# Three more 4 KB tiles from a smaller descriptor memory, and new tables for the first 224 steps of a diffusion-transformer kernel

## The chip, the cores and the metric

The kernel runs on one core of a Trainium2 chip. TensorE (PE) multiplies, VectorE (DVE) and ScalarE (ACT) work on tiles, GpSimd (POOL) and SyncE (SP) start transfers. The metric is the device time of one execution in microseconds (us), given as the median of three runs. A profile of one execution comes with it.

## The reference

One layer of a hybrid diffusion transformer is computed in fp32 for two groups of 128 tokens (a prompt and a sample), with D = 2048 and D_FF = 8192:

- adaLN: (shift1, scale1, gate1, shift2, scale2, gate2) = SiLU(c) @ w_ada + b_ada, one vector per group
- h = RMSNorm(x) * (1 + scale1) + shift1; one projection p = h @ w_in gives q, k, v of two attention mixers and two gates
- mixer A (windowed, grouped heads) and mixer B (neighbourhood attention with a position bias), both also over cached keys
- merged = sigmoid(gate_A) * (o_A @ w_br_a) + sigmoid(gate_B) * (o_B @ w_br_b); x = x + gate1 * (merged @ w_out)
- x = x + gate2 * (relu(h2 @ w_up)^2 @ w_down), with h2 from RMSNorm, shift2 and scale2

## The kernel before

**Steps.** All large products are cut into some 450 steps. A step has one weight tile of 128x1024 fp32 (512 KB). SP loads it (`raw`, L255), ACT copies it into a rounded high part `wH` (`copy`, L103, called from `prep`), DVE subtracts to get the low part `wL` (L281), and PE runs 12 matmuls of 128x512: high x high, low weight x high, and high x low of the activations, for two token groups and two slices of the contraction. The matmul lines differ by stage: L599 to L601 in the first three steps, L463 to L465 in `start_steps`, L498 to L500 in `products`, L332 to L334 later. Steps are counted from 0 here.

**Order.** Nothing is scheduled at run time. `run` (L305) writes the program out step by step: before step i it issues the loads of the steps up to i + RUN[i], prepares (`prep_to`) the tiles up to step i + LOOK[i], writes the 12 matmuls, and then the functions that `at` has hung on step i. Each engine runs its own instructions in the order in which they were written, so a digit of LOOK decides how many subtractions DVE has ahead of what step i hangs on it. LO_DMA lists steps whose `wL` comes another way: ACT copies `wH` with a factor of -1 and POOL starts a transfer that adds the weights to it (L287, L288).

**What is hung on the steps.** `mod_pair` (five groups of adaLN columns; the first, in `begin`, is narrower) loads eight tiles `araw` of 512 KB, multiplies them with the conditioning vector on PE (`wide_mm`, L366) into one PSUM bank, has ACT copy the sum to `S` (`ada_evac`), and PE transposes `S` four times (`ada_cols`, L380, `ps_sel`). One step later `make_h` and one more later `split_h` make the activations of the next slice. DOTS and its kin place dot products on DVE (L1499, two of them to a tile `aT`) for the other adaLN columns. POST, JOBS and SS_AT place the work of the attention.

**Chunks.** The input projection begins while only some slices of h are known: `start_steps` runs each unit of 512 columns over a chunk of h and puts the partial sum away. SEED1 says for each unit and chunk how the parts are joined: "1" lets ACT copy the earlier part into the PSUM banks beforehand (a seed), "0" lets DVE add it afterwards (L476). The sums live in pairs of banks from a pool of four (`pacc`, L87), so a step that opens a new sum takes a pair that one of the last two sums held, and waits until that has been copied or added away.

**Tiles.** Weights, their two parts, `araw`, `aT` and most activations are tiles of 4 KB per partition. They come from one pool with GEN = 50 rotating buffers under one tag.

Of the kernel before, what the change touches and what calls it, by code (L numbers as in the profile page):

```python
# [10 lines left out]
F32 = mybir.dt.float32  # L11
F32R = mybir.dt.float32r
# [18 lines left out]
GEN = 50  # L31
# [4 lines left out]
FILL = {1: [("gB", 2), ("gB", 3)], 3: [("gB", 0), ("gB", 1)]}  # L36
DOTS1 = [9, 11, 14, 19, 22, 24, 25, 27, 28, 30, 32, 33, 34, 35, 37, 40, 41, 42, 44, 46, 48, 49, 51, 53]
# [9 lines left out]
SEED1 = "111110100100111111011111111001011111"  # L47
# [4 lines left out]
LO_DMA = [50, 54, 56, 63, 77, 107, 129, 144, 145, 176, 184, 188, 189, 203, 228, 233, 250, 286, 297, 360, 388, 392, 403, 447]  # L52
LO_AHEAD = 2

LOOK = "610013015100121312024402233324102425654224523344556654121016645565652437574377445343425661516353205100022636320000411134203644154134500458230315565645456443574337324421522555644666784051000205311111322534111433455554321045445111013410444324654734331001335565775443654453304436533423355423455542233213213545587654334232213213202440122544412433432313432443523324313211333435533333213331314344422557756822145342656433332302254541454475574464555546763333345544"
RUN = "345110004667224234111350007998421004464200022565595544243214333434399864346555377654224635443144230021224242114401324515201346530331035587986564665545676867644543555342013141147676676965699967265287998988511453877787785653022200123446553345324545104653232464345673321110102122521121211202355533232133432223443232410110000000011234344212022112531112752123301000112323643331133410100122454235566436675432012021222210010001154457832224556577677636445664422134"
CONST_AT = [83, 79]
XL_DMA = [8]
HI_DMA = []
ADA_AT = [None, 4, 13, 22, 25]  # L60
XS_AT = {1: 3, 2: 24, 3: 34}
POST = {('kvA', 0): [81, 83, 89], ('qA', 0): [84, 86, 92], ('qA', 1): [84, 86, 90], ('kB', 0): [88, 92, 98], ('qB', 0): [94, 100, 104], ('kB', 1): [98, 101, 103], ('qB', 1): [102, 106, 107]}
JOBS = [[93, 94, 95, 100, 106], [93, 94, 99, 104, 106], [98, 98, 100, 105, 114], [101, 104, 107, 110, 111], [107, 107, 110, 115, 118], [109, 109, 111, 118, 121], [113, 114, 115, 126, 128], [116, 116, 119, 122, 124]]
# [9 lines left out]
M_AT = [4, 6, 9]  # L73
# [7 lines left out]
def tile_hybrid_step(ctx: ExitStack, tc: tile.TileContext, a):  # L81
# [20 lines left out]
    def copy(out, in_):  # L102
        act.activation(out, in_, AF.Copy)  # L103
# [6 lines left out]
    cols = cp.tile([P, 172], F32, name="cols")[:, 0:164]  # L110
# [20 lines left out]
    wr = G("wr", F32R)  # L131

    def warm_r(*forms):

        for m, v in forms:
            pe.matmul(ps_warm[0:m, 0:v.shape[-1]], wr[:, 0:m], v, start=True, stop=True)

# [11 lines left out]
    for h in range(2):  # L149
        copy(wr[:, 512 * h:512 * h + 512], wm)  # L150
# [154 lines left out]
    def run():  # L305
        loads.sort(key=lambda x: x[:2])
        for st in wsteps:
            while loads and loads[0][0] <= st["i"] + int(RUN[st["i"]]):
                loads.pop(0)[2]()
# [3 lines left out]
            to = st["i"] + int(LOOK[st["i"]]) + 1  # L313
# [255 lines left out]
    def begin():  # L569
# [49 lines left out]
        warm_r(*[(P, wr[:, 0:512])] * 3, *[(P, wr[:, 8:520])] * 3)  # L619
# [1060 lines left out]
```

## Time and profile before

| | |
|---|---|
| runs | 1313.8, 1313.86, 1314.27 us, median 1313.86 us |
| profiled execution | 1313.68 us, of which the span is 1311.8 us |
| PE busy | 1298.4 us (99%) |
| DVE busy | 1146.1 us (87%) |
| ACT busy | 917.5 us (70%) |
| POOL busy | 58.5 us (4%) |
| mean read and write rate | 300 GB/s |

Times in the profile count from the start of the span. The 1.9 us between the span and the execution lie outside it. A row of the view over time gives start, duration, engine, line, operation, output <- inputs, shape and count, and in brackets how long the engine had been idle and which instruction ended that. Rows of the view of waits give an instruction, what it waited for, the sum in us, how often, and the longest. A window row gives the window, its length, and for each engine the busy time and the number of instructions, then the granted clock of PE, the busy share of the DMA engines and the rate. The 128x512 matmuls are pipelined: a row shows 0.39 us for one, but the next starts 0.227 us later, so a step of 12 takes 2.72 us.

### The profile page before, as it was taken

How to read it: one execution, taken by the hardware profiler on the slowest of the kernel's cores; microseconds unless marked ns; L12 is line 12 of the kernel's file. 1: busy time of each engine (PE TensorE's matmuls, PEld its weight loads, DVE VectorE, ACT ScalarE, POOL GpSimd, SP SyncE). 2: the span in 40 equal slices, each digit the busy share in tenths (PEclk: the TensorE clock that was granted, in tenths of full speed). 3: DMA queues.
4: the chain of work that ended last, by engine and by line, in shares of the span. 5: the costliest groups of instructions: out<-in, count | busy, mean ns of one | idle time of the engine just before them, and what ended most of it. 6: DMA issues, size and time to landing. Idle time of an engine off the chain costs nothing.

```text
span 1311.8 us, 17435 instructions
## 1 busy us (share of the span) xinstructions
PE 1298.4 (99%) x5978; PEld 1052.2 (80%) x5978; DVE 1146.1 (87%) x1532; ACT 917.5 (70%) x1289; POOL 58.5 (4%) x67
## 2 busy tenths in 40 slices
PE   8999999999999999999999999999999999999998
PEld 4767888888777778888888888888888888888886
DVE  4578999999899999999879998897989999979653
ACT  5657766689765657645687857869678787796881
POOL 0000000341100000000000000000000000000000
PEclk9999999999999999999999999999999999999999
DMA  9999998897889999999399775788586696968692
GB/s 379 418 411 420 361 365 320 306 364 278 290 347 365 419 384 330 369 344 372 113 321 317 244 256 179 273 293 282 201 297 224 212 317 248 297 161 304 204 345 78
DMA packets 148313, 393.80 MB, mean 300 GB/s; under 512 B 51680, under 2 KB 52672, under 8 KB 148224
## 3 DMA queue, kind: packets, MB, share of 16 engines
q1 hardware_dynamic: 144064, 378.18, 77.7%
q0 software_dynamic: 4016, 14.42, 5.7%
q8 instruction: 47, 0.77, 0.2%
q14 instruction: 42, 0.34, 0.1%
q10 hardware_dynamic: 144, 0.08, 0.0%
HBM read 373.97 MB, written 8.70 MB: 292 GB/s over the span
## 4 chain that ended last, share of the span: by engine, by line
PE 70%; DVE 3%; ACT 0%; issue 0%; DVEq 0%; ACTq 0%
PE acc L332 14%; PE acc L333 14%; PE acc L334 14%; PE Q L1281 6%; PE Q L1283 6%; PE Q L1282 6%; PE Z L1281 1%; PE Z L1283 1%; PE Z L1282 1%; DVE aT L1499 1%; DVE junk L1499 1%; PE acc L1119 1%; PE acc L1120 1%; PE acc L1102 1%; PE acc L1101 1%; PE acc L1103 1%
## 5 line engine op out<-in xcount | busy, mean ns | idle before, releaser
L281 DVE TENSOR_TENSOR wL<-raw,wH 128x1024 fp32r<-128x1024 f32 x361 | 425.7, 1224 | 62.4 <-ACT wH L103 61.8
L103 ACT ACTIVATE wH<-raw 128x1024 fp32r<-128x1024 f32 (+1 forms) x391 | 387.4, 1043 | 49.7 <-PE acc L334 10.2
L1499 DVE SCALAR_TENSOR_TENSOR aT<-aT,cB 128x1024 f32<-128x1024 f32 x144 | 173.9, 1224 | 1.1
L1499 DVE SCALAR_TENSOR_TENSOR junk<-aT,cB 128x1024 bf16<-128x1024 f32 x144 | 173.9, 1224 | 0.0
L463 PE MATMUL acc<-wH,hH 128*128 128x512 f32 x276 | 108.2, 392 | 0.0
L465 PE MATMUL acc<-wH,hL 128*128 128x512 f32 x276 | 107.5, 389 | 0.0
L464 PE MATMUL acc<-wL,hH 128*128 128x512 f32 x276 | 107.5, 389 | 0.0
L103 ACT ACTIVATE uH<-raw 128x1024 fp32r<-128x1024 f32 x34 | 36.1, 1063 | 65.7 <-DVE raw L1345 57.9
L463 PEld LDWEIGHTS acc<-wH,hH 128*128 128x128 f32 x276 | 51.8, 188 | 13.8 <-issue 2.5
L465 PEld LDWEIGHTS acc<-wH,hL 128*128 128x128 f32 x276 | 51.8, 188 | 10.9
L464 PEld LDWEIGHTS acc<-wL,hH 128*128 128x128 f32 x276 | 51.8, 188 | 10.6
L103 ACT ACTIVATE tH<-t 128x1024 fp32r<-128x1024 f32 x34 | 36.0, 1058 | 28.7 <-DVE t L1338 26.5
L332 PE MATMUL acc<-wH,hH 128*128 128x512 f32 x128 | 52.6, 411 | 0.0
L333 PE MATMUL acc<-wL,hH 128*128 128x512 f32 x128 | 50.1, 392 | 1.3 <-DVE wL L281 1.3
L498 PE MATMUL acc<-wH,hH 128*128 128x512 f32 x128 | 50.5, 394 | 0.0
L499 PE MATMUL acc<-wL,hH 128*128 128x512 f32 x128 | 49.9, 390 | 0.1
L334 PE MATMUL acc<-wH,hL 128*128 128x512 f32 x128 | 50.1, 391 | 0.0
L500 PE MATMUL acc<-wH,hL 128*128 128x512 f32 x128 | 50.0, 390 | 0.0
L1348 DVE TENSOR_TENSOR uL<-raw,uH 128x1024 fp32r<-128x1024 f32 x34 | 41.7, 1226 | 1.4 <-ACT uH L103 0.3
L103 ACT ACTIVATE acc<-dsum 128x512 f32<-128x512 f32 x56 | 31.7, 590 | 15.7 <-DVE t L1067 8.3
L1338 DVE TENSOR_TENSOR t<-raw 128x1024 f32<-128x1024 f32 x34 | 41.4, 1219 | 1.3 <-PE Q L1282 1.3
L1347 DVE TENSOR_TENSOR tL<-t,tH 128x1024 fp32r<-128x1024 f32 x34 | 41.4, 1219 | 0.0
(652 smaller groups left out, 3331.9 us busy)
## 6 DMA issues: line engine op xcount, KB each, us to landing
raw<-in_w_in SPq DMA_DIRECT2D x133, 512.0 KB, 7.6
raw<-in_w_down SPq DMA_DIRECT2D x128, 512.0 KB, 6.3
aT<-in_w_adaT SPq DMA_DIRECT2D x80, 512.0 KB, 8.0
raw<-in_w_upF SPq DMA_DIRECT2D x68, 512.0 KB, 5.4
aT<-in_w_gT SPq DMA_DIRECT2D x64, 512.0 KB, 7.7
raw<-in_w_up SPq DMA_DIRECT2D x60, 512.0 KB, 6.2
araw<-in_w_pair SPq DMA_DIRECT2D x48, 512.0 KB, 8.9
raw<-in_w_out SPq DMA_DIRECT2D x32, 512.0 KB, 9.2
```

Of the source, the lines that this page charges most:

```text
L103: act.activation(out, in_, AF.Copy)
L281: dve.tensor_tensor(st["lo"], st["raw"], st["hi"].bitcast(F32), op=OP.subtract)
L332: pe.matmul(acc[tb], sh, wh[:, k, :], start=f, stop=False, skip_group_check=seeded)
L333: pe.matmul(acc[tb], sh, wl[:, k, :], start=False, stop=False, skip_group_check=seeded)
L334: pe.matmul(acc[tb], sl, wh[:, k, :], start=False, stop=l, skip_group_check=seeded)
L463: pe.matmul(acc[tb], sh, wh[:, k, :], start=opened[u] and k == 0, stop=False, skip_group_check=skip)
L464: pe.matmul(acc[tb], sh, wl[:, k, :], start=False, stop=False, skip_group_check=skip)
L465: pe.matmul(acc[tb], sl, wh[:, k, :], start=False, stop=last and k == 1, skip_group_check=skip)
L1281: pe.matmul(acc, stat[0], hi, start=f, stop=False)
L1282: pe.matmul(acc, stat[0], lo, start=False, stop=False)
L1283: pe.matmul(acc, stat[1], hi, start=False, stop=l)
L1499: dve.scalar_tensor_tensor(out, box["raw"], 1.0, cB[s, tag], op0=OP.mult, op1=OP.mult, accum_out=dst[:, s, fb:fb + 1])
```

## The change

- The memory that POOL uses for the descriptors of its transfers is set to 4096 bytes per partition. It was left at its default before. That frees space for three more tiles of 4 KB: GEN is 53.
- SLOTS, a string of one letter for each tile in the order in which the tiles are allocated, writes down in which of the 53 places each tile lies. Every place is a tag of its own with one buffer.
- The tables of the first 224 steps get other values: LOOK, RUN (now with digits up to 35), SEED1, DOTS, DOTS1, LO_DMA (24 steps as before, 15 instead of 14 of them among the first 224), POST, JOBS, XS_AT, M_AT, CONST_AT, PREP_IN.
- A group of adaLN columns is no longer loaded and multiplied in one go. ADA gives for each of its four pairs of tiles the step of the load and the step of the matmuls, and then the steps of the transposes, `make_h` and `split_h`. SS does the same for a group in the attention.
- The six fp32r matmuls on a tile `wr` that keep PE busy in `begin`, and the two ACT copies that fill this tile, are gone; six bf16 matmuls of the kind used before them stand there.

```diff
+SLOTS = 'ABCDEFGHIJKLMNOPQRSTUVWXYZabcdefghijklmnopqrstuvwxyz0GHIJ...
-GEN = 50
+GEN = 53
+SCRATCH = 4096
...
-SEED1 = "111110100100111111011111111001011111"
+SEED1 = "010010101101111110101110011111111110"
...
-LO_DMA = [50, 54, 56, 63, 77, 107, 129, 144, 145, 176, 184, 188, 189, 203, 228, 233, ...
+LO_DMA = [50, 54, 57, 63, 77, 107, 118, 126, 132, 142, 144, 184, 188, 189, 203, 233, ...
-LOOK = "6100130151001213120244022333241024256...
-RUN = "34511000466722423411135000799842100446...
+LOOK = "5111220650321366544500401233313002424...
+RUN = "96834416112255307530055100224400200469...
-ADA_AT = [None, 4, 13, 22, 25]
-XS_AT = {1: 3, 2: 24, 3: 34}
+ADA = {1: [[1, 2, 3, 5], [0, 2, 4, 5], [5, 5, 5]], 2: [[13, 14, 15, 18], [11, 14, 16, 17], [18, 19, 20]], 3: [[17, 18, 18, 22], [17, 18, 21, 21], [21, 21, 27]], 4: [[24, 26, 26, 26], [25, 27, 27, 27], [28, 29, 30]]}
+XS_AT = {1: 1, 2: 19, 3: 20}
...
-SS_AT = [118, 127]
+SS = [[[117, 119, 122, 126], [116, 119, 125, 127], 129]]
...
+    def slot():
+        return {"tag": "g" + next(slots), "bufs": 1} if SLOTS else {"tag": "g"}
+
     def G(name, dt=F32):
-        return gp.tile([P, 1024], dt, name=name, tag="g")
+        return gp.tile([P, 1024], dt, name=name, **slot())
...
-        i = ADA_AT[f]
-        for j in range(2):
-            load_at(i, lambda j=j: wide_load(box, 0, f, j))
-            at(i, lambda j=j: wide_mm(box, j))
-        at(i, lambda: ada_evac(box))
-        at(i + 1, lambda: ada_cols(box, 0, k0, 2))
-        at(i + 2, lambda: make_h(k0, 2))
-        at(i + 3, lambda: split_h(k0, 2))
+        come, go, (c, m, s) = ADA[f]
+        for j in range(4):
+            load_at(come[j], lambda j=j: wide_load(box, 0, f, j))
+            at(go[j], lambda j=j: wide_mm(box, j))
+        at(go[3], lambda: ada_evac(box))
+        at(c, lambda: ada_cols(box, 0, k0, 2))
+        at(m, lambda: make_h(k0, 2))
+        at(s, lambda: split_h(k0, 2))
...
-        warm_r(*[(P, wr[:, 0:512])] * 3, *[(P, wr[:, 8:520])] * 3)
+        warm(6)
...
-    nc = bacc.Bacc("TRN2", target_bir_lowering=False, num_devices=1)
+    nc = bacc.Bacc("TRN2", target_bir_lowering=False, num_devices=1, dynamic_dma_scratch_size=SCRATCH)
```

The change moves instructions on every engine. Three places are shown, where line numbers of the changed kernel are lower by two than those before.

**PE, the first group of adaLN columns.** Before, after the 60 matmuls of steps 0 to 4, all eight tiles are multiplied in one go (the last matmul of step 4, the visit, the first of step 5); the transposes of `S` follow one step later:

```order
L465 MATMUL acc_421<-wH_342,hL0_249 128x512
L366 MATMUL ps_ada_437<-araw_372,rt_91 32x512 x2
L366 MATMUL ps_ada_437<-araw_374,rt_91 32x512 x2
L366 MATMUL ps_ada_437<-araw_376,rt_91 32x512 x2
L366 MATMUL ps_ada_437<-araw_378,rt_91 32x512 x2
L366 MATMUL ps_ada_437<-araw_380,rt_91 32x512 x2
L366 MATMUL ps_ada_437<-araw_382,rt_91 32x512 x2
L366 MATMUL ps_ada_437<-araw_384,rt_91 32x512 x2
L366 MATMUL ps_ada_437<-araw_386,rt_91 32x512 x2
L463 MATMUL acc_464<-wH_355,hH0_248 128x512
```

Now four of the tiles stand behind step 2, ahead of the first matmul of step 3:

```order
L599 MATMUL acc_303<-wH_263,hL0_254 128x512
L364 MATMUL ps_ada_401<-araw_183,rt_90 32x512 x2
L364 MATMUL ps_ada_401<-araw_185,rt_90 32x512 x2
L364 MATMUL ps_ada_401<-araw_189,rt_90 32x512 x2
L364 MATMUL ps_ada_401<-araw_191,rt_90 32x512 x2
L461 MATMUL acc_413<-wH_334,hH0_253 128x512
```

and the last two behind step 5, with the transposes right after them:

```order
L463 MATMUL acc_460<-wH_360,hL0_254 128x512
L364 MATMUL ps_ada_401<-araw_379,rt_90 32x512 x2
L364 MATMUL ps_ada_401<-araw_381,rt_90 32x512 x2
L378 MATMUL ps_sel_482<-ident_92,S_480 128x128 x4
L461 MATMUL acc_498<-wH_430,hH0_253 128x512
```

One visit became three, behind steps 2, 4 and 5, and the step between the visit and the transposes is gone.

**SP, the first loads of whole tiles.** Before, five weight tiles and then the eight tiles of the group:

```order
L255 DMA raw_188<-in_w_in 128x1024
L196 DMA silu_151<-srow_224 32x128
L255 DMA raw_366<-in_w_in 128x1024
L356 DMA araw_372<-in_w_pair2 128x1024
L356 DMA araw_374<-in_w_pair2 128x1024
```

Now the group's tiles stand between the weights:

```order
L253 DMA raw_179<-in_w_in 128x1024
L253 DMA raw_181<-in_w_in 128x1024
L354 DMA araw_183<-in_w_pair2 128x1024
L354 DMA araw_185<-in_w_pair2 128x1024
L253 DMA raw_187<-in_w_in 128x1024
L354 DMA araw_189<-in_w_pair2 128x1024
L354 DMA araw_191<-in_w_pair2 128x1024
L253 DMA raw_193<-in_w_in 128x1024
L194 DMA silu_148<-srow_229 32x128
```

The group's first four tiles are the 3rd, 4th, 6th and 7th whole tile to be loaded instead of the 6th to 9th; the last (`araw_381`) is the 14th instead of the 13th.

**DVE, step 14.** Step 14 belongs to unit kB, block 0, in both programs, and its partial sum is added by DVE in both. Before, two subtractions stand ahead of the two halves of this addition, one of them for step 14's own tile:

```order
L281 TENSOR_TENSOR wL_684<-raw_534,wH_682 128x1024
L281 TENSOR_TENSOR wL_688<-raw_536,wH_686 128x1024
L476 TENSOR_TENSOR u_kB0_478<-u_kB0_478,acc_727 128x512
L476 TENSOR_TENSOR u_kB0_478<-u_kB0_478,acc_728 128x512
L1499 SCALAR_TENSOR_TENSOR junk_743,shT0_153<-aT_540,cB0_390 128x1024
```

Now LOOK[14] is 6 instead of 1, and four subtractions for steps 17 to 20 stand directly ahead of it:

```order
L279 TENSOR_TENSOR wL_722<-raw_523,wH_720 128x1024
L279 TENSOR_TENSOR wL_726<-raw_642,wH_724 128x1024
L279 TENSOR_TENSOR wL_730<-raw_650,wH_728 128x1024
L279 TENSOR_TENSOR wL_734<-raw_652,wH_732 128x1024
L474 TENSOR_TENSOR u_kB0_473<-u_kB0_473,acc_736 128x512
L474 TENSOR_TENSOR u_kB0_473<-u_kB0_473,acc_737 128x512
```

The addition has moved behind tiles that are needed three to six steps later.

More of the change, by code (lines that the diff above doesn't have):

```diff
@@ L72 @@
 M_TE = (3,)
-M_AT = [4, 6, 9]
+M_AT = [2, 4, 10]
 FLIP = 1
@@ L91, in tile_hybrid_step @@
     act, dve, pe, pool, sync = nc.scalar, nc.vector, nc.tensor, nc.gpsimd, nc.sync
+    slots = iter(SLOTS)
+    def slot():
+        return {"tag": "g" + next(slots), "bufs": 1} if SLOTS else {"tag": "g"}
     def G(name, dt=F32):
-        return gp.tile([P, 1024], dt, name=name, tag="g")
+        return gp.tile([P, 1024], dt, name=name, **slot())
     def SM(n, name):
@@ L107, in split @@
         dve.tensor_tensor(lo, full, hi.bitcast(F32), op=OP.subtract)
-    cols = cp.tile([P, 172], F32, name="cols")[:, 0:164]
+    cols = cp.tile([P, 172], F32, name="cols")[:, :164]
     act.dma_start(cols, a["cols"])
@@ L130, in tile_hybrid_step @@
     dve.memset(onef, 1.0)
[L131 to L136, printed above, removed]
     pw = cp.tile([P, 32], F32, name="pw")
@@ L148, in tile_hybrid_step @@
     act.activation(first, pw[:, 0:1], AF.Sigmoid)
-    for h in range(2):
-        copy(wr[:, 512 * h:512 * h + 512], wm)
     def rsqrt(out, in_, add, by=None):
@@ L307, in run @@
         for st in wsteps:
-            while loads and loads[0][0] <= st["i"] + int(RUN[st["i"]]):
+            while loads and loads[0][0] <= st["i"] + int(RUN[st["i"]], 36):
                 loads.pop(0)[2]()
@@ L312, in run @@
                     fn()
-            to = st["i"] + int(LOOK[st["i"]]) + 1
+            to = st["i"] + int(LOOK[st["i"]], 36) + 1
             while by_dma and by_dma[0] < to + LO_AHEAD:
@@ L350, in pair_mm_q, with wide_load, wide_mm @@
                       start=j == 0 and q == 0, stop=(j == 1 or alone) and q == 3, tile_position=(0, 32 * k))
-    def wide_load(box, nsub, f, half):
-        for q in range(4 * half, 4 * half + 4):
+    def wide_load(box, nsub, f, j):
+        for q in (2 * j, 2 * j + 1):
             box[q] = G("araw")
             sync.dma_start(box[q], a["w_pair2"][nsub, f][:, 1024 * q:1024 * q + 1024])
-    def wide_mm(box, half):
-        if half == 0:
+    def wide_mm(box, j):
+        if j == 0:
             box["ps"] = bank("ps_ada")
-        for q in range(4 * half, 4 * half + 4):
+        for q in (2 * j, 2 * j + 1):
             raw = box.pop(q).rearrange("p (k n) -> p k n", k=2)
@@ L554, in tile_hybrid_step @@
     for g, i in XS_AT.items():
-        assert all(i < ADA_AT[f] + 2 for f in (2 * g, 2 * g + 1) if f < FB1 // 2)
+        assert all(i < ADA[f][2][1] for f in (2 * g, 2 * g + 1) if f < FB1 // 2)
         at(i, lambda g=g: x_scale(g))
@@ L971, in halves @@
     def halves(key, name):
-        return gp.tile([P, 2048], U16, name=f"{name}{key[0]}{key[1]}", tag="g")
+        return gp.tile([P, 2048], U16, name=f"{name}{key[0]}{key[1]}", **slot())
     def part(key, src):
@@ L1570, in tile_hybrid_step @@
         box = {}
-        for j in range(2):
-            i = SS_AT[2 * c + j]
-            load_at(i, lambda box=box, c=c, j=j: wide_load(box, 1, c, j))
-            ex(i, lambda box=box, j=j: wide_mm(box, j))
-        ex(i, lambda box=box: ada_evac(box))
-        ex(i + 1, lambda box=box, c=c: ada_cols(box, 1, 2 * c, 2))
-    assert i + 1 <= end_of(("out", 2)), (i, end_of(("out", 2)))
+        come, go, i = SS[c]
+        for j in range(4):
+            load_at(come[j], lambda box=box, c=c, j=j: wide_load(box, 1, c, j))
+            ex(go[j], lambda box=box, j=j: wide_mm(box, j))
+        ex(go[3], lambda box=box: ada_evac(box))
+        ex(i, lambda box=box, c=c: ada_cols(box, 1, 2 * c, 2))
+    assert i <= end_of(("out", 2)), (i, end_of(("out", 2)))
     g2 = list(zip(DOTS2, [(("g2", n % KC), n // KC, n // KC) for n in range(2 * KC)], strict=True))
```

21 lines of the change are left out of this document (11 added, 10 removed).

## The prediction

> **What bounds the kernel now.** I read the view of waits for PE first, then windows of the span. Waits:
>
> ```profile
> PE acc L333 <- DVE wL L281: 1.3, 2, 0.8
> PE ps_o L918 <- ACT probT L103: 1.2, 1, 1.2
> ...
> PE ps_gr L1520 <- DVE gc_g L1505: 0.8, 1, 0.8
> PE ps_sel L380 <- ACT S L103: 0.6, 1, 0.6
> PE ps_ada L366 <- DMA araw<-in_w_pair: 0.4, 2, 0.2
> PE ps_PT L911 <- ACT T_qB L820: 0.3, 1, 0.3
> ```
>
> Windows (length, then busy time of PE, PEld, DVE, ACT and POOL, granted clock, DMA share, GB/s):
>
> ```profile
> 25.00:50.00 25.00, 24.25 (x116) 16.28 (x117) 12.56 (x19) 16.53 (x27) 0.00 (x0) 1.00 1.03 418
> 50.00:100.00 50.00, 49.87 (x252) 36.36 (x251) 34.65 (x46) 31.47 (x47) 0.00 (x0) 1.00 1.03 414
> 300.00:500.00 200.00, 196.30 (x977) 159.40 (x976) 192.33 (x306) 135.72 (x283) 11.34 (x12) 1.00 0.94 350
> 500.00:1200.00 700.00, 700.00 (x3109) 579.43 (x3108) 635.91 (x775) 513.88 (x587) 14.60 (x19) 1.00 0.80 271
> ```
>
> PE is the bound. From 500 to 1200 us it is never idle, and the tables there are the old ones. What new tables can win is PE's idle time ahead of that: 0.75 us in the second window, 0.13 in the third and 3.7 in the attention. There is no reserve in the clock, which is 1.00 throughout. Of all these waits only 0.4 us are for a transfer, so three more tiles, which let loads start earlier, have almost nothing to win by themselves. The other side of the ledger is what the new order adds to PE.
>
> **The change part by part.** *First group of columns.* The view over time of PE:
>
> ```profile
> 29.51 0.39 PE L463 MATMUL acc<-wH,hH 128*128 128x512 f32 x1
> ...
> 39.98 1.05 PE L366 MATMUL ps_ada<-araw,rt 128*32 128x512 f32 x4 [0.25 <-DMA araw<-in_w_pair]
> 40.97 0.50 PE L463 MATMUL acc<-wH,hH 128*128 128x512 f32 x1
> ...
> 43.82 0.60 PE L380 MATMUL ps_sel<-ident,S 128*128 128x128 f32 x4
> 44.18 0.48 PE L463 MATMUL acc<-wH,hH 128*128 128x512 f32 x1
> ```
>
> Step 3 starts at 29.51. The visit behind step 4 is paced by loads: PE waits for its last tile, the 13th whole tile, which is in at 39.9, and at 418 GB/s a tile takes 0.524 MB / 418 GB/s = 1.25 us. So the k-th tile is in at 39.9 - 1.25 x (13 - k). Now four tiles stand ahead of step 3, the 7th among them, which is in at 32.4; from the last tile's start to the next step take 40.97 - 39.98 = 1.0, so step 3 starts at 33.4, and two steps of 2.72 end at 38.9.
>
> The cost of a visit comes from two undisturbed ones, a whole and a half group:
>
> ```profile
> 65.84 0.39 PE L465 MATMUL acc<-wH,hL 128*128 128x512 f32 x1
> 66.16 3.64 PE L366 MATMUL ps_ada<-araw,rt 128*32 128x512 f32 x32
> 69.73 0.50 PE L463 MATMUL acc<-wH,hH 128*128 128x512 f32 x1
> ...
> 427.92 0.39 PE L334 MATMUL acc<-wH,hL 128*128 128x512 f32 x1
> 428.24 1.92 PE L366 MATMUL ps_ada<-araw,rt 128*32 128x512 f32 x16
> 430.09 0.50 PE L332 MATMUL acc<-wH,hH 128*128 128x512 f32 x1
> ```
>
> 69.73 - 65.84 = 3.89 and 430.09 - 427.92 = 2.17; each holds one matmul's own 0.227, and the first matmul after a visit is 0.11 late (40.97 and 44.18 show 0.50 and 0.48 instead of 0.39). So a whole visit costs 3.77 and a half 2.05, which is 0.43 for a tile and 0.33 for the interruption. The visit of two tiles behind step 4 takes 1.2, step 5 ends at 42.8, the last visit at 44.0 (the 14th tile is in at 41.2). Now `ps_sel` follows at once. The nearest row is the same wait in the beginning, with a half-width `S`:
>
> ```profile
> 14.81 0.36 ACT L103 ACTIVATE S<-ps_ada 128x256 f32<-128x256 f32 x1
> 15.22 0.44 PE L380 MATMUL ps_sel<-ident,S 128*128 128x128 f32 x2 [0.62 <-ACT S L103]
> 69.87 0.60 ACT L103 ACTIVATE S<-ps_ada 128x512 f32<-128x512 f32 x1 [2.85 <-PE ps_ada L366]
> ```
>
> With 0.60 instead of 0.36 it is 0.86 (between 0.6, were the copy as short, and 1.5, behind one ACT copy of 0.6). With the transposes' 0.36 step 6 starts near 45.2 instead of 44.18: **+1.0** (0 to +1.8).
>
> *The other groups.* Up to step 29 PE is interrupted 12 times instead of 8 by visits and transposes; the first group has one of the four more, the others 3 x 0.33 = **+1.0** (0, if an interruption is hidden, to 1.3). Group 3 also has its transposes in the step of its last visit: 0.86 and 0.11 for the late matmul, **+0.95** (0 to 1.6). The wait at 76.32 (below) goes: **-0.3**.
>
> *Step 14.* DVE and ACT before, and PE two steps on, where the pair of banks is wanted again:
>
> ```profile
> 72.11 1.37 DVE L476 TENSOR_TENSOR u_kB<-u_kB,acc 128x512 f32<-128x512 f32 x2 [4.61 <-PE acc L465]
> 75.04 3.50 DVE L281 TENSOR_TENSOR wL<-raw,wH 128x1024 fp32r<-128x1024 f32 x3
> 70.36 1.11 ACT L103 ACTIVATE acc<-u_kB 128x512 f32<-128x512 f32 x2
> 71.41 2.94 ACT L103 ACTIVATE wH<-raw 128x1024 fp32r<-128x1024 f32 x3
> 75.37 1.28 ACT L103 ACTIVATE u_kB<-acc 128x512 f32<-128x512 f32 x2 [1.02 <-PE acc L465]
> 75.80 0.39 PE L498 MATMUL acc<-wH,hH 128*128 128x512 f32 x1
> 76.32 0.50 PE L499 MATMUL acc<-wL,hH 128*128 128x512 f32 x1
> ```
>
> Before, DVE had idled 4.61 us when the addition came up, and added at once. Now four subtractions stand ahead. Count from the end of step 13 on PE. ACT copies that step's sum away (1.28, begun 0.43 before the step's end), writes two seeds (1.11) and the first `wH` (about 1.0): 3.0. Four subtractions at (3.50 - 1.22) / 2 = 1.14 end at 7.5, and half of the addition, 0.69, at 8.2. PE needs that pair for step 16, after two steps and a visit of two tiles: 2 x 2.72 + 1.2 = 6.6. It waits 1.5: **+1.5**. Bounds: 0, were the four subtractions done beforehand, and 2.2, were the whole addition waited for. What is late next is step 16 and all behind it. At two places a new sum takes the pair that the step directly before has left, and PE waits for ACT's copy: it ends at 75.37 + 0.60 = 75.97, 0.17 after the next step's start at 75.80, plus 0.11 for the late matmul, **+0.55** for both (0 to 1).
>
> By step 30 PE is 1.0 + 1.0 + 0.95 - 0.3 + 1.5 + 0.55 = 4.7 us later than before.
>
> *Attention.* It has 24 interruptions instead of 26: -0.6. The waits on `wL` (1.3, two places) and `probT` (1.2) go, since by the order lists what they wait for stands earlier against PE's matmuls: with 0.11 for each late matmul **-2.8** (0 to -4.1, if `ps_PT` and `ps_gr` went too). But DVE has hardly a gap:
>
> ```profile
> 100.00:470.00 370.00, 359.10 (x556) 1.00 0.93 347
> ```
>
> SEED1 has more zeros: 16 halves added by DVE instead of 10, each (1.37 - 0.69) = 0.68, so 4.1 us, less one subtraction of 1.14 that POOL takes over: +2.9 on DVE until `ps_gr`, where PE waits for DVE already. PE arrives there 4.7 - 0.6 - 2.8 = 1.3 later, so 1.6 come back as waits (0, if DVE's 10.9 us of gaps absorb them, to 2.9): **+1.6**. Further on, until the new tables end, DVE is as full, and late subtractions there can cost **+0.5** (0 to 1.0).
>
> *Costed at nothing:* the two `wr` copies (ACT idles in the beginning), six bf16 matmuls for six fp32r ones, SLOTS (the loads stay ahead of PE; were that cover gone, a load would cost its 1.25), and the smaller descriptor memory (a rival, below).
>
> **Sum:** 4.7 - 0.6 - 2.8 + 1.6 + 0.5 = +3.4. The profiled execution took 1313.68, which gives 1317.1; the median of the runs is 0.2 higher, so 1317.3.
>
> **The rivals.** *DVE absorbs (no change).* The waits of the attention all go (-4.1), DVE's work vanishes in its 10.9 us of gaps: 4.7 - 0.6 - 4.1 = 0, 1313.9. For it: subtractions may run ahead more freely with more tiles. Against: `ps_gr` hangs on the last dot product, which nothing moves. *Cheap visits (faster).* The interruptions cost nothing and `S` is there in time: of the early terms step 14's 1.5, the 0.55 and the -0.3 remain, and with -0.6 and -4.1 it is -2.9, 1311.0. Against: both prices have rows. *More waits (slower still).* None of the attention's waits goes, and step 14 and the two waits for `S` take their upper bounds (0.7, 0.65 and 0.65 more): 4.7 + 2.0 - 0.6 + 0.5 = +6.6, 1320.5. *The descriptor memory.* One mechanism from one point: if 4 KB hold one transfer, POOL's second one must wait for the first.
>
> ```profile
> 579.58 0.85 POOL L288 DMA_DIRECT2D wL<-in_w_out  x1 [4.04 <-ACT wL L287]
> 582.57 0.85 POOL L288 DMA_DIRECT2D wL<-in_w_out  x1 [2.13 <-ACT wL L287]
> wL<-in_w_out POOLq DMA_DIRECT2D x4, 512.0 KB, 10.0
> ```
>
> These two start 3 us apart and take 10, so they overlap; in series the later `wL` would be 7 late, some 5 us at the pair of steps 142 and 144, 1322. Against: one such tile is 128 rows over 16 engines, a small count. [...] *The clock.* Short waits could bring the clock down. The row of 25 to 50 us has 0.75 us of idle time at 1.00. [...] If it fell to half for some 4 us, that were +2, 1319.3.
>
> **How the numbers follow.** Forecast 0.60, with its own range 1315.4 to 1319.3; DVE absorbs 0.18; cheap visits 0.08; more waits 0.09; descriptor memory 0.03; clock 0.02. A measurement tells 0.2% from nothing, 2.6 us, so slower begins at 1316.5 and faster ends at 1311.2. Slower: five sixths of the forecast, with the last three cases, 0.64. Faster: the cheap visits and a little of DVE absorbs, 0.10. Same: 0.26. The range reaches down into "DVE absorbs" and up to "more waits": 1312.8 to 1320.7.
>
> **What would show it.** After: step 3 starts near 33.4; `ps_sel` waits for `S` two times more, 0.86 each; L498 (now L496) near 77 us waits 1.5 us for DVE; the waits of L333 and L918 are gone; `ps_gr` waits longer than 0.8. From 500 us on the two programs run in parallel. I am wrong if PE is less than 3 us late at step 30, or if the waits at `ps_gr` stay at 0.8.

## The result, and the profile after

| | before | changed |
|---|---|---|
| runs in this comparison, us | 1313.61 to 1314.27, median 1313.83 | 1323.19, 1326.40, 1330.91, 1336.37, median 1328.66 |
| profiled execution, us | 1313.68, span 1311.8 | 1330.91, span 1329.0 |
| ratio | | 1.0115, 95% interval 1.009 to 1.0141 |

The change makes the kernel slower by 14.8 us. Slower was forecast, but by 3.4. And something is new that the kernel before does not have: its executions agree within 0.7 us, those of the changed kernel lie 13 us apart.

The page of the changed kernel, its head and the row of PE and the other engines:

```profile
span 1329.0 us, 17381 instructions
...
PE 1308.7 (98%) x5978; PEld 1053.2 (79%) x5978; DVE 1150.0 (87%) x1538; ACT 911.2 (69%) x1275; POOL 61.2 (5%) x67
```

PE is busy 10.3 us longer with as many matmuls (1298.4 before), so some of them ran slower. The view of waits for PE (what waits, for what, sum in us, times, longest):

```profile
PE Q L1280 <- DMA XL<-in_w_upF: 2.4, 1, 2.4
PE ps_sel L378 <- ACT S L110: 2.1, 3, 0.7
PE Q L1279 <- ACT up L1186: 1.8, 1, 1.8
PE ps_gr L1518 <- DVE gc_g L1503: 1.7, 1, 1.7
...
PE ps_qT L812 <- DVE u_kvA L789: 1.1, 1, 1.1
PE acc L496 <- DVE u_kB L474: 1.0, 1, 1.0
PE ps_qT L812 <- DVE u_kvA L799: 0.9, 1, 0.9
PE ps_ada L364 <- DMA araw<-in_w_pair: 0.8, 2, 0.6
```

Two of these (`ps_sel`, `acc L496`) stand in the forecast by name and roughly by size, `ps_gr` by name. Four do not: the two at `ps_qT` and the two at `Q`, the longest of all. The windows of the prediction (length, then busy time of PE, PEld, DVE, ACT, POOL, granted clock, DMA share, GB/s), now for the changed kernel:

```profile
25.00:50.00 25.00, 23.16 (x110) 14.85 (x111) 11.56 (x19) 16.36 (x27) 0.00 (x0) 1.00 1.03 419
50.00:100.00 50.00, 48.97 (x237) 33.24 (x239) 34.63 (x45) 28.45 (x39) 0.00 (x0) 1.00 1.03 419
300.00:500.00 200.00, 197.70 (x989) 160.59 (x988) 187.09 (x296) 142.50 (x295) 13.89 (x14) 1.00 0.94 352
500.00:1200.00 700.00, 695.52 (x3066) 573.55 (x3065) 629.07 (x773) 501.07 (x572) 12.93 (x17) 0.99 0.78 262
```

The last row holds the surprise. Before, PE was busy 700.00 of these 700 us; now it idles 4.5 us there, and the clock is 0.99.

To see where the time goes, take the start of the same matmul in both traces and subtract. The changed program is behind by, at the start of a step:

| step | begins before at, us | behind, us | what lies between |
|---|---|---|---|
| 3 | 29.5 | 4.0 | four tiles of adaLN ahead of it |
| 6 | 44.2 | 1.2 | first group done |
| 16 | 75.8 | 1.1 | |
| 30 | 122.9 | 5.4 | all adaLN groups, step 14, waits for PSUM |
| 88 | 280.7 | 5.4 | nothing |
| 92 | 293.3 | 9.2 | the waits at `ps_qT`, half clock |
| 142 | 469.7 | 6.7 | rest of the attention |
| 144 | 476.3 | 7.6 | `ps_gr` |
| 200 | 631.4 | 8.6 | small steps of 0.5, 0.2 and 0.4 |
| 216 | 676.8 | 8.6 | |
| 230 | 714.9 | 17.1 | one place, 8.5 us |
| 400 | 1177.5 | 17.2 | the old tables |

So four sums make the 17.2 us of the profiled execution: 5.4 in the beginning, 2.1 from there to `ps_gr`, 1.0 up to step 200, and 8.5 between steps 216 and 230. The rest is 0.2.

**The place at 690 us.** There SP transposes the planes of the first piece of `up` by a DMA (`flip`, L985, L987 before). The view over time of SP, before and after (start, duration, engine, line):

```profile
660.47 2.51 SPq L987 DMA_TRANSPOSE pTa<-pla  x1
```

```profile
670.71 8.58 SPq L985 DMA_TRANSPOSE pTa<-pla  x1
679.35 1.04 SPq L1194 DMA_DIRECT2D x1d<-x  x2
```

Its issue holds SP for 8.58 us, and the loads behind it in SP's program wait. The view of the tile `pTa` in the changed kernel, then those of `XL`, the low half that POOL's accumulating DMA makes, and of `aT`, the last load ahead of the transpose (issued at 666.91):

```profile
L110 ACT ACTIVATE fTa<-pTa x1: 2500/2500/2500, 688.4 to 688.4; 128x2048 uint16<-128x2048 uint16 x1
...
  DMA pTa<-pla: 8.1, 1
...
DMA to landing us min/median/max: 17.6/17.6/17.6
```

```profile
L286 POOL DMA_DIRECT2D XL<-in_w_upF x1: 934/934/934, 674.9 to 674.9; - x1
...
DMA to landing us min/median/max: 13.2/13.2/13.2
```

```profile
L1484 SPq DMA_DIRECT2D aT<-in_w_gT x1: 328/328/328, 666.9 to 666.9; - x1
...
DMA to landing us min/median/max: 12.3/12.3/12.3
```

`aT` lands at 666.9 + 12.3 = 679.2, and 0.1 later SP is free again: the transpose is issued only when the last load in flight has landed. Then it lands at 670.7 + 17.6 = 688.3, and `XL` at 674.9 + 13.2 = 688.1. Nothing else lands between 679.2 and these two. The same holds for every transpose in all fourteen profiles that finds three or more of SP's loads in flight, 78 in number (seven before, five in the change): its issue ends within 0.3 us of the landing of the last of them. Before, the transpose took 5.8 us and `XL` 9.4:

```profile
L288 POOL DMA_DIRECT2D XL<-in_w_upF x1: 935/935/935, 665.6 to 665.6; - x1
...
DMA to landing us min/median/max: 9.4/9.4/9.4
```

PE waits 2.4 us for `XL`, and 1.8 for `up`: ACT had idled 8.1 us for the transpose at the head of its program and is late with PE's next sums. What these waits do to PE's clock (windows of the changed kernel):

```profile
670.00:679.00 9.00, 9.00 (x41) 7.48 (x40) 7.46 (x9) 7.88 (x9) 0.93 (x1) 1.00 1.07 302
679.00:688.00 9.00, 6.79 (x30) 5.28 (x29) 2.89 (x3) 1.26 (x2) 0.00 (x0) 0.99 1.25 144
688.00:698.00 10.00, 7.98 (x18) 5.76 (x19) 4.83 (x7) 9.05 (x10) 0.00 (x0) 0.50 0.55 224
698.00:708.00 10.00, 10.00 (x46) 8.26 (x45) 8.99 (x11) 7.85 (x10) 0.00 (x0) 1.00 0.61 166
```

For 10 us the granted clock is 0.50. Of the 8.5 us, 2.4 + 1.8 = 4.2 are waits, and the 4.3 left go with matmuls 0.427 us apart instead of 0.227. And in the stretch ahead of it the DMA engines are busy by the profile (1.25) but move 144 GB/s.

### The profile page after: what moved, and what is told of

Same layout as the page of the kernel before. It is cut to its first block, busy times and chain, and to the rows that moved or that the text cites. A ratio compares the mean times of both kernels' runs of the same rounds, so it can differ in the third digit from the quotient of the medians.

```text
span 1329.0 us, 17381 instructions
## 1 busy us (share of the span) xinstructions
PE 1308.7 (98%) x5978; PEld 1053.2 (79%) x5978; DVE 1150.0 (87%) x1538; ACT 911.2 (69%) x1275; POOL 61.2 (5%) x67
## 4 chain that ended last, share of the span: by engine, by line
PE 68%; DMA 6%; DVE 4%; issue 1%; ACT 1%; SPq 0%; DVEq 0%; ACTq 0%
PE acc L330 12%; PE acc L331 12%; PE acc L332 12%; PE Q L1279 6%; PE Q L1280 6%; PE Q L1281 6%; DMA aT<-in_w_adaT 3%; DVE wL L279 2%; DMA raw<-in_w_br_a 1%; DMA pTa<-pla 1%; PE acc L497 1%; PE acc L498 1%; PE acc L496 1%; DVE junk L1497 1%; PE ps_S L859 1%
## 5 line engine op out<-in xcount | busy, mean ns | idle before, releaser
L462 PEld LDWEIGHTS acc<-wL,hH 128*128 128x128 f32 x276 | 51.8, 188 | 10.7 <-DVE wL L279 0.4
L110 ACT ACTIVATE tH<-t 128x1024 fp32r<-128x1024 f32 x34 | 36.0, 1058 | 29.5 <-DVE t L1336 26.7
L496 PE MATMUL acc<-wH,hH 128*128 128x512 f32 x128 | 51.4, 401 | 1.0 <-DVE u_kB L474 1.0
L110 ACT ACTIVATE fTa<-pTa 128x2048 uint16<-128x2048 uint16 x16 | 40.4, 2527 | 8.1 <-DMA pTa<-pla 8.1
```

The costliest lines, as they stand in the source:

```text
L462: pe.matmul(acc[tb], sh, wl[:, k, :], start=False, stop=False, skip_group_check=skip)
```

## The experiments

Three questions were open: do the tiles or the memory matter at all, what makes the place at 690 us, and what the 5.4 us and the waits in between come to. Theory A says that the tables alone make the loss; the rivals blame the memory (B) or the tiles (C).

### Memory and tiles

The kernel before with the memory of the change alone, and with three more rotating tiles besides:

```diff
-    nc = bacc.Bacc("TRN2", target_bir_lowering=False, num_devices=1)
+    nc = bacc.Bacc("TRN2", target_bir_lowering=False, num_devices=1, dynamic_dma_scratch_size=4096)
```

> The kernel before with the descriptor memory of 4096 bytes alone (50 rotating tiles, tables as before). Theory A, that the loss comes from the changed tables (5.3 us by step 30 and 8.4 us at the first transpose of a piece of up): the same as before, 1313.8 within 1 us, and the wL of POOL land after 9 us as before. Rival B, that the smaller descriptor memory delays POOL's accumulating DMAs: over 1316, with POOL's issues later and the one beside the first transpose of up near the 13.2 us of the change.

Measured: 1313.89 us (1313.63 to 1314.59), ratio 1.0001, interval 0.9991 to 1.0011. The smaller memory costs nothing; rival B is out.

```diff
-GEN = 50
+GEN = 53
```

> The kernel before with the smaller descriptor memory and three more rotating tiles (53), tables as before. Theory A: 1312.5 to 1314.5, since PE waits for no load in the kernel before and the order of the loads around the transposes is unchanged. Rival C, that loads that start sooner (more tiles) collide with the transposes: a wait of PE over 1 us behind a transpose, and 1318 or more, with runs that lie several us apart.

Measured: 1314.63 us (1314.51 to 1314.97), ratio 1.0005, interval 0.9996 to 1.0014: 0.1 above what was expected, and nothing that can be told from no change. The transpose is issued within 1.61 us, and PE loses nothing behind it: it is 1.2 us behind the kernel before at step 200 and at step 236. Rival C in its plain form is out: more tiles do not bring the collision.

The changed kernel with its tiles taken in turn:

```diff
-SLOTS = 'ABCDEFGHIJKLMNOPQRSTUVWXYZabcdefghijklmnopqrstuvwxyz0GHIJ...
+SLOTS = ''
```

> The changed kernel with its 53 tiles taken in turn instead of by the written-down places; all tables as changed. If the places are worth something, PE waits for wL or wH appear that the change does not have (I expect some 3 to 5 us of them in attention, where tiles are scarcest): 1330 to 1335. If the collision at the first transpose of up comes from the tables, it stays (the transpose takes over 12 us); if it comes from the places, the transpose goes back to under 6 us and the time falls by up to 8 us.

Measured: 1326.43 us (1326.26 to 1326.97), less than expected. The written-down places are worth something: this kernel is 10.7 us behind at step 160, where x4 below, with the places, is 6.3 behind, with waits that the changed kernel does not have (the longest 1.8 us for `oLB` and 0.8 for `probT`). But at 690 us it loses only 1.1. The transpose still stands behind the loads:

```profile
673.99 7.60 SPq L985 DMA_TRANSPOSE pTa<-pla  x1
```

It takes 12.0 us in all, `XL` 8.2, and PE waits 0.2 for `up`; no stretch at half clock follows. So the collision comes from the tables, but its size is not fixed by them: here the same rows lie a few us apart and it is nearly hidden.

### The order of loads and transpose

RUN decides how far the loads run ahead. In the changed kernel six more loads stand ahead of the first transpose of `up`. Taking the digits of steps 200 to 224 from the kernel before puts them behind it. Here and below, edits of a part of a table are written as assignments. (The letters of SLOTS are given out by the tile's name in this kernel, so that each tile keeps its place in the other order.)

```diff
-RUN[200:225] = "8dcb5205a6cad566385656244"
+RUN[200:225] = "8988511453877787785653022"
```

> The changed kernel with the digits of RUN for steps 200 to 224 as before, so that six loads (three of weights, two of cB, one of aT) stand behind SP's first transpose of up instead of ahead of it; nothing else differs. Theory A: the transpose is issued within 4 us and lands within 8 us instead of 17.6, PE's waits of 2.4 and 1.8 us near 690 us go, and with them the half clock behind them: 8 us less in the profiled run, 1319 to 1321, and the runs lie closer together than the 13 us of the change. Rival C (more tiles or their places make the queue stall whatever the order): the transpose still takes over 12 us, 1326 or more.

Measured: 1322.55 us (1320.98 to 1322.75), 6.1 less than the changed kernel, and the runs lie 1.8 us apart instead of 13. SP in this kernel:

```profile
669.38 1.61 SPq L985 DMA_TRANSPOSE pTa<-pla  x1
```

It lands after 3.7 us, PE no longer waits there, and the clock is 1.00 between 670 and 700 us. The profiled execution (1320.98, span 1319.1) has the 8 us that were expected: 7.3 us behind at step 200 and 7.2 at step 230. The median is 1.6 us above it and above the range expected, as much as one stretch at half clock costs (below); that it is that, no profile shows.

Is it the waiting for the loads, or POOL's DMA beside it? In the next kernel the loads stand ahead as in the change, but DVE makes `XL`:

```diff
-XL_DMA = [8]
+XL_DMA = []
```

> The changed kernel, with the one low half (XL) that POOL's accumulating DMA makes beside the first transpose of up made by DVE instead (one subtraction of 1.2 us more on DVE, XL_DMA empty); the six loads still stand ahead of the transpose. Theory A2, that the 17.6 us are two things added, 8.6 us until the loads ahead have landed and some 7 us in which the transpose and POOL's DMA hold each other up: the transpose lands after 10.5 to 11.5 us, as the first of m does behind seven loads, and PE waits there for less than 1 us: 1321 to 1324. Rival A3, that POOL's DMA only lands late because the queue is held: the transpose still takes over 15 us and the time stays at 1326 or more.

```profile
669.45 8.99 SPq L985 DMA_TRANSPOSE pTa<-pla  x1
...
690.85 1.62 SPq L985 DMA_TRANSPOSE pTa<-pla  x1
```

Measured: 1322.48 us (1321.17 to 1323.23). The issue is as long as in the change, 8.99 us, but the transpose lands 2.0 us later, after 11.0, and PE does not wait. Theory A2 holds: two things were added, the wait for the loads and, when POOL's accumulating DMA is started in between, some 7 us more (17.6 instead of 8.6 + 2.0). The size of the second differs: from the end of the issue to the landing it is 9.0 us in the change, 7.1 in x11 below and 4.4 in x3, the three runs in which POOL's DMA starts meanwhile, and 1.7 to 3.7 for all other transposes. Either alone costs PE next to nothing: this kernel and x4 take the same time, and its PE loses 0.7 us at step 236.

And the other way round: is the order of the loads enough, in a program whose early tables are those of before? The pair is x12 below.

```diff
-RUN[200:225] = "8988511453877787785653022"
+RUN[200:225] = "8dcb5205a6cad566385656244"
```

> The tables as before and 53 tiles at places written for them, with the gate row's transpose one step later, and one thing of the change: the digits of RUN for steps 200 to 224, by which the six loads stand ahead of the first transpose of up. Its pair x12 has these digits as before. Theory A, that the order of the loads alone is enough: the transpose takes over 12 us, and PE waits behind it for 1 us or more: 3 to 9 us above x12. Rival A4, that the early start of the loads (the changed tables ahead of step 200) is needed too: the transpose takes 8 to 12 us, PE does not wait, within 0.5 us of x12.

```profile
659.12 9.43 SPq L985 DMA_TRANSPOSE pTa<-pla  x1
```

```profile
PE Q L1279 <- ACT up L1186: 3.8, 1, 3.8
```

Measured: 1317.92 us (five runs: 1317.14, 1317.88, 1317.92, 1321.79, 1321.95) against 1312.45 for x12, so 5.5 us for 25 digits, in the middle of what theory A expected. The transpose takes 16.5 us. In the profiled execution PE is 1.4 us ahead of the kernel before at step 216, and 4.2 behind at step 230.

### The beginning

x4 with all early tables as before (LOOK and RUN of steps 0 to 59, DOTS1, SEED1, XS_AT, and each group in one visit), its places written anew for this order:

```diff
-ADA = {1: [[1, 2, 3, 5], [0, 2, 4, 5], [5, 5, 5]], 2: [[13, 14, 15, 18], ...
+ADA = {1: [[4, 4, 4, 4], [4, 4, 4, 4], [5, 6, 7]], 2: [[13, 13, 13, 13], ...
```

> x4_loads_behind with the early part as before: the digits of LOOK and RUN for steps 0 to 59, DOTS1, SEED1, XS_AT, and each adaLN group in one visit at its step of before (the places of the tiles written anew for this order). Theory A: the 5.3 us that the changed kernel is behind from step 30 on are the early tables' alone, and nothing later pays them back: 1315.5 to 1317.5, against 1322.5 of x4. Rival: the later tables were made for the later start, so that waits of DVE's work come back in attention; then the time stays above 1319.

Measured: 1317.75 us (1316.12 to 1318.61), 4.8 less than x4. The upper end of the range just misses it. In its profiled execution (span 1315.4) PE is 0.3 us behind at step 30 instead of 5.5, and 3.6 at the end instead of 7.3: of 5.2 us 3.7 are kept. The other 1.5 are lost again between steps 130 and 144, half of it at one wait, as the rival said they might:

```profile
PE ps_gr L1518 <- DVE gc_g L1503: 2.5, 1, 2.5
```

PE comes there 4.4 us sooner than in x4, DVE's `gc_g` only 3.7 (475.7 us instead of 479.4), so the wait grows from 1.7 to 2.5.

Two parts alone, both on x4. The four groups in one visit each, at the step of their last visit:

```diff
-ADA[1][1], ADA[2][1], ADA[3][1], ADA[4][1] = [0, 2, 4, 5], [11, 14, 16, 17], [17, 18, 21, 21], [25, 27, 27, 27]
+ADA[1][1], ADA[2][1], ADA[3][1], ADA[4][1] = [5, 5, 5, 5], [17, 17, 17, 17], [21, 21, 21, 21], [27, 27, 27, 27]
```

> x4_loads_behind with the four adaLN groups' matmuls in one visit each, at the step of the last of the four visits; their loads stay where they are (the places of the tiles written anew). My forecast priced the twelve extra interruptions at some 0.33 us each on top of what is waited for: 1 to 2 us less than x4, 1320.5 to 1321.5. Rival: the interruptions are hidden and the waits for S set the time: within 0.5 us of x4.

```profile
PE ps_gr L1518 <- DVE gc_g L1503: 2.4, 1, 2.4
PE acc L496 <- DVE u_kB L474: 2.1, 1, 2.1
```

Measured: 1323.01 us (1321.83 to 1324.52), no less than x4, so for the time the rival holds, though not for its reason: the interruptions are not hidden. (They fall from 12 in all to 6, so the forecast's price for the difference is 6 x 0.33 = 2.0, not that of twelve.) PE is 3.9 us behind at step 30 instead of 5.5. That is with a wait at L496 of 2.1 us instead of 0.96, since PE comes there earlier. From step 130 to 144 it then loses 4.0 us, where x4 loses 1.0: the wait at `ps_gr` is 0.7 longer, seven matmuls behind it run at half clock (1.4), and 0.8 are lost just ahead. DVE's `gc_g` is there at 479.3 us, as in x4 (479.4). Where DVE is the later one and does not gain as well, a gain of PE is lent, not given.

LOOK of step 14, the digit that the forecast singled out:

```diff
-LOOK[14] = 6
+LOOK[14] = 1
```

> x4_loads_behind with LOOK of step 14 at 1 as before instead of 6, so that four subtractions of DVE stand behind the add that PE waits for at step 16. My forecast gave these +1.5 us; the profile of the changed kernel has a wait of 0.96 us there. Expected: the wait goes to 0.1 or less and nothing gives it back: 1321.2 to 1322. Rival: DVE is behind everywhere in this part, and the wait comes back within ten steps: 1322.5.

Measured: 1320.17 us (1319.70 to 1321.10), below the range expected. In the profiled executions the span is 1318.0 instead of 1319.1: 1.1 less, and the wait at L496 is gone. That is the wait's 0.96 and the late matmul's 0.1. `gc_g` comes 1.2 us sooner as well (478.2), so the wait at `ps_gr` stays at 1.7 and the gain is kept. The medians are 2.4 apart, more than this wait can explain; the rest may lie in stretches at half clock that one execution has and the next has not (mean clocks of 0.998 to 0.999 in x4's executions, 0.998 to 1.0 here), but no profile shows it.

### The clock

How long may PE wait until its clock goes down? The change and x4 each have an answer, and they do not agree. The same two waits at `ps_qT`, in the profiled execution of the change and of x4 (view over time of PE):

```profile
290.11 0.41 PE L812 MATMUL ps_qT<-ident,u_kvA 128*128 128x128 f32 x2 [1.08 <-DVE u_kvA L789]
291.43 0.41 PE L812 MATMUL ps_qT<-ident,u_kvA 128*128 128x128 f32 x2 [0.91 <-DVE u_kvA L799]
291.60 0.52 PE L496 MATMUL acc<-wH,hH 128*128 128x512 f32 x1
291.92 0.63 PE L497 MATMUL acc<-wL,hH 128*128 128x512 f32 x1
292.34 0.63 PE L498 MATMUL acc<-wH,hL 128*128 128x512 f32 x1
```

```profile
290.34 0.41 PE L812 MATMUL ps_qT<-ident,u_kvA 128*128 128x128 f32 x2 [1.24 <-DVE u_kvA L789]
291.66 0.41 PE L812 MATMUL ps_qT<-ident,u_kvA 128*128 128x128 f32 x2 [0.91 <-DVE u_kvA L799]
291.83 0.48 PE L496 MATMUL acc<-wH,hH 128*128 128x512 f32 x1
292.14 0.40 PE L497 MATMUL acc<-wL,hH 128*128 128x512 f32 x1
292.38 0.40 PE L498 MATMUL acc<-wH,hL 128*128 128x512 f32 x1
```

In the first the next eight matmuls start 0.427 us apart, 8 x 0.2 = 1.6 us lost; in the second, with a longer wait, 0.24. So the length alone does not decide. A kernel with pauses of three lengths asks how much it decides:

```diff
+    def pause(n):
+        ps = bank("ps_x")[:, 0:P]
+        pe.matmul(ps, pxb, pxb, start=True, stop=True)
+        for _ in range(n):
+            pool.memset(px, 0.0)
+        pe.matmul(ps, pxb, pxb, start=True, stop=True)
...
             prep_to(to)
+            if st["i"] in PAUSE:
+                pause(PAUSE[st["i"]])
             st["mm"](st)
```

> The kernel before with fourteen pauses of PE, three steps apart from step 31 on: two small matmuls into a bank of PSUM, and between them POOL fills a tile of 4 KB per partition once, twice or three times (waits of PE of some 1.2, 2.1 and 3.0 us, taken in turn); the descriptor memory at 4096 makes room. Nothing else waits there, so the time grows by the pauses, 27 to 30 us. Theory C1, that a wait beyond some length puts the clock to half: the matmuls behind the long pauses start 0.427 us apart instead of 0.227 for some us, all five or none of a length. Rival C2, that it depends on where the wait falls: pauses of one length are followed by half clock in some places and not in others, the longer the oftener.

Measured: 1361.74 us (one run), 48 more than before instead of 27 to 30. The waits add up to 33.1 us (two of them were 4.1 and 4.4 us, since POOL was busy with transfers), the half clock makes 9.6 of the rest, the small matmuls and the late first matmul behind each pause the others (0.36 us a pause). Windows behind a wait of 1.1 us (at 160.9), of 2.1 (137.9, and 210.7) and of 3.1 (149.6):

```profile
138.00:142.00 4.00, 4.00 (x19) 3.31 (x19) 3.96 (x8) 1.64 (x3) 0.00 (x0) 1.00 0.92 336
150.00:154.00 4.00, 4.00 (x12) 3.13 (x11) 4.00 (x5) 0.00 (x0) 0.00 (x0) 0.57 0.67 272
161.00:165.00 4.00, 4.00 (x19) 3.31 (x19) 0.00 (x0) 1.66 (x3) 0.00 (x0) 1.00 0.73 246
...
211.00:215.00 4.00, 4.00 (x12) 3.14 (x12) 3.79 (x13) 0.00 (x0) 0.00 (x0) 0.61 0.00 1
```

| wait of PE | places | followed by half clock | matmuls 0.427 us apart |
|---|---|---|---|
| 1.1 us | 4 | 0 | |
| 2.1 us | 5 | 2 | 7, 6 |
| 3.1 to 4.4 us | 5 | 5 | 8, 8, 7, 7, 5 |

C2 holds: the longer the oftener, and two waits of 2.14 us differ. The half clock sets in 0.6 to 1.5 us after the wait, and the longest stretches are 8 x 0.427 = 3.4 us.

Where a wait falls can be read from the record of the granted clock. In all fourteen profiles, between the clock's first rise and the end of PE's work, every stretch at half clock begins a whole number of 3.413 us steps after that rise and lasts one step or, in the change at 687.8 us, three. (In the change the rise is at 5.165 us and the stretches begin at 291.885 and 687.831, 84 and 200 steps later.) Cut PE's time into these steps, and look at those at full clock: behind all eleven in which PE idles 1.93 us or more the next step is at half clock, and behind none with 1.79 us or less. (In the change 1.99 and 2.04 us of idle PE stand ahead of the two stretches, and no other step at full clock has more than 1.40; before, none has more than 1.22.) The windows of these steps around the waits at `ps_qT`, first in the change, then in x4:

```profile
288.47:291.89 3.42, 1.43 (x8) 0.81 (x7) 3.35 (x8) 3.17 (x6) 1.07 (x2) 1.00 1.03 420
291.89:295.30 3.41, 3.41 (x9) 2.64 (x8) 3.41 (x4) 3.02 (x5) 0.00 (x0) 0.50 1.02 388
```

```profile
286.58:289.99 3.41, 2.52 (x12) 1.74 (x10) 3.34 (x7) 3.41 (x6) 0.02 (x1) 1.00 1.03 420
289.99:293.41 3.42, 2.16 (x11) 1.71 (x12) 3.35 (x7) 3.12 (x7) 1.07 (x2) 1.00 1.03 408
```

In the change both waits fall into one step, with 3.42 - 1.43 = 2.0 us idle; in x4 they fall into two, with 0.9 and 1.3. So it is with the five waits of 2.14 us: two lie almost whole in one step (2.14 and 2.12), three are cut by its edge (at most 1.5 in one step). The first rise comes 3.8 to 10.1 us after the start of the span (3.83 before, 5.17 in the change), at another time in each of the fourteen, so I take it that where the edges fall is chance. Why the half clock in the change goes on for three steps, with 0.9 and 1.3 us idle in the first two, stays open.

Such chance would explain a part of the scatter: one program's waits would fall into these steps otherwise in each execution. The four executions of the changed kernel had mean granted clocks of 0.999, 0.998, 0.995 and 0.993, in the order of their times. From 0.999 to 0.993, 0.6% of 1330 us, is 8 us by my estimate; the other 5 of the 13 would be longer waits, which no profile of the slowest execution is there to show.

### The waits in the attention and at the gate

x7 with two waits taken away by putting PE's part later:

```diff
-POST = {('kvA', 0): [81, 86, 88], ...
+POST = {('kvA', 0): [81, 86, 90], ...
...
-    ex(i, lambda: gate_rows("g1"))
+    ex(i, lambda: dot_sum(gcol["g1"], "g1", 2))
+    ex(i + 1, lambda: gate_rows("g1", False))
```

> x7_look14 with two waits of PE taken away by putting PE's part later, not the work it waits for earlier: the transposes of kvA at step 90 instead of 88 (waits of 1.2 and 0.9 us), and the transpose for the first gate row one step behind the additions of DVE (1.7 us). Theory D, that PE sets the time here: 3.5 us less than x7's 1320.2, 1316 to 1317, and the runs closer together, since the waits that can put the clock to half are gone. Rival, that DVE sets the time in attention: the 2.1 us of kvA come back as later waits for DVE's work, and only the gate's 1.7 us are won: 1318 to 1319.

```profile
PE ps_S L859 <- ACT T_qA L818: 2.2, 1, 2.2
```

Measured: 1319.42 us (1317.47 to 1319.56). The waits at `ps_qT` and `ps_gr` are gone, but a new one of 2.2 us stands a few steps on, for ACT's copies of the transposed q, which now come later. Behind it PE is 6.1 us behind at step 96, where x7 is 6.7: of 2.1 us 0.6 are won. The rival is right that the wait comes back, though what is waited for is ACT, not DVE; the median lies 0.4 above its range. The gate keeps its gain: from step 142 to 144 this kernel wins 1.1 us on the kernel before, where x7 loses 0.9. The runs did not come closer together; a wait of 2.2 us is left.

What helps at the gate helps the kernel before too, which waits 0.8 there. The changed program with all tables as before, 53 tiles at places written for them, and the second edit above:

> The tables as before, 53 tiles at places written for them, the smaller descriptor memory, and PE's transpose for the first gate row one step behind the additions that it waits for (before: a wait of 0.82 us). The wait goes and nothing behind it gives it back, since PE waits for nothing of a size later on: 1312.8 to 1313.3, against 1313.9 of the kernel before. Rival: the three more tiles let loads start sooner as in x2 and cost the 0.7 us again: 1313.8.

Measured: 1312.45 us (ten runs, 1312.24 to 1312.84), ratio to the kernel before 0.9989, interval 0.9979 to 0.9999. It is below both kernels, and a little below what was expected. From step 142 to 144 it wins 1.1 us, the wait and the late matmul, and keeps it to the end (1.4 ahead at step 400). The three tiles do no harm when their places fit.

## Why the prediction was right and wrong

It was right on the sign, for reasons that were in part the true ones, and wrong on the size: 17.2 us in the profiled execution, 14.8 in the medians, instead of 3.4. The sign was not luck: without the part that was not foreseen the kernel is still 8.7 us slower than before (x4, medians). By its steps:

**The beginning** (+4.7 by step 30) measured 5.4. Step 3 starts at 33.5, forecast 33.4. The first group is 1.2 late at step 6, forecast 1.0. `ps_sel` waits two more times, 0.74 and 0.72, forecast 0.86. The wait of step 14 is 0.96 at 76.9 us, forecast 1.5; x7 shows that the digit of LOOK is its cause. x5 shows that the early tables as a whole are.

**Attention** (-0.6 - 2.8 + 1.6 = -1.8) measured +2.1 from step 88 to 144. The waits of L333 and L918 went as forecast, and `ps_gr` grew, by 0.9 (forecast 1.6). What failed is the sentence that the waits go "since by the order lists what they wait for stands earlier": it was asked of the waits that were there, and no new ones were looked for. POST had moved the rotation of `kvA` on DVE from step 83 to 86, while PE's transposes of it moved from 89 to 88. That makes 2.0 us of waits, and half clock behind them 1.6 more in the profiled execution; in x4, without the half clock, the same stretch is +0.8. "DVE +2.9" was nearly right: DVE is busy 3.9 us longer, and not in x5, which has the old SEED1.

**Later on** (+0.5) measured 1.0, its upper bound.

**Costed at nothing.** The memory: right (x1). "SLOTS (the loads stay ahead of PE)": here is the step that failed by the most. The loads did stay ahead of PE. They stood ahead of a DMA transpose as well, which waited 8.58 us for the six in flight, and "from 500 us on the two programs run in parallel" took for granted that nothing of the new tables mattered there, though they reach to step 224, near 699 us before. The queue that six loads had been moved past, SP's, was not read. Its price is 8.5 us of the profiled execution, 6.1 in the medians (x4), and 5.5 with the old tables ahead of it (x11).

**The clock** was a rival at 0.02 with +2 us for some 4 us at half clock, an estimate that no run shows. What the runs showed: in the profiled execution of the change the half clock lasts 3.4 us at 292 and 10.2 at 690, and takes 1.6 and 4.3 us, 5.9 us together. There is a wait of 2.4 us, and 1.93 us idle in one step of 3.413 us were enough; at 292 two waits of 1.08 and 0.91 make it up.

**The other rivals.** "DVE absorbs" found support in one thing, that a gain of PE can end at `ps_gr` (all of it in x6, a part in x5, none in x7), but the beginning costs what it costs. "Cheap visits" is out: x6 finds the interruptions' price, 1.6 us by step 30. "More waits" has the right kind of mechanism and the wrong places.

Not settled: how the 5.4 us of the beginning divide, beyond what x6 and x7 show, between the waits for `S` and those for PSUM pairs; and why the collision takes 12.0 us in x3, 16.5 in x11 and 17.6 in the change, with five, six and six loads in flight.

## What to carry to other kernels

When a table lets loads run further ahead, read the queue that issues them and not only the engine that uses them: something that waits for the loads ahead of it, here a DMA transpose, can be late by what was put there (its issue took 8.58 us behind six loads, 1.61 in x4 with none). A gain of PE ahead of a place where it waits for another engine is kept only as far as that engine gains too; look for the last such wait first, since moving PE's part of it by a step is worth more (1.1 us for one line) than what is won ahead of it. And add up PE's waits that lie within 3.4 us of each other: here 1.08 and 0.91 us cost a stretch at half clock, 1.6 us, in the change, and 1.24 and 0.91 cost none in x4, which by my estimate makes a part of the scatter.

## What the runs showed of the hardware

- With three or more of SP's loads in flight, a DMA transpose on SP's queue held the queue until they had landed: 7.60 us behind five loads (x3), 8.58, 8.99 and 9.43 behind six (the change, x9, x11), against 1.61 with none (x4); the issue ended within 0.3 us of the last landing in 78 of 78. SP issued nothing meanwhile: in the change nothing between 670.71 and 679.35 us.
- Where an accumulating DMA of POOL started while the transpose was held, the transpose landed late: 17.6, 16.5 and 12.0 us after its start (the change, x11, x3) instead of 11.0 without that DMA (x9). The accumulating DMA itself took 13.2, 11.1 and 8.2 us, against 9.4 to 10.6 in the runs where the transpose was not held behind six loads; so it was late in two of the three. In the change 144 GB/s were moved in all from 679 to 688 us, where the profile shows the DMA engines as full (1.25).
- The granted clock went to half in steps of 3.413 us counted from its first rise, which came at 3.83 us before, at 5.17 in the change and between 3.8 and 10.1 in all: behind all eleven steps at full clock with 1.93 us or more of idle PE, behind none with 1.79 or less. A stretch of one step cost up to 1.6 us (eight matmuls 0.427 us apart instead of 0.227). By single waits in x8: after 1.1 us in none of four places, 2.1 in two of five, 3.1 and more in five of five.
